# A Hymba layer on one core: one product taken apart, fillers in other PSUM tiles, a shared tile, a split reciprocal, and one hand-over between engines

## The chip, the core and the metric

The kernel runs on one core of a Trainium2 chip. The metric is device time of one execution in microseconds (us). Of each kernel there are several timed runs, of which the median counts, and one execution that was profiled.

## What is computed

One layer of a network with attention and a state-space scan side by side, over 1024 tokens of 1024 features, in float32:

```python
x = LN0(alpha*x + 0.5*SwiGLU_1(x))
u = x @ W_in            # [q | k | v | z | x_ssd | B | C | dt_fwd | dt_bwd]
a = attention(rms+rotary(q), rms+rotary(k), v)    # 8 query heads of 64, 2 key/value heads, all tokens
xs, B, C = silu(conv5(x_ssd, B, C))               # centred depthwise convolution along tokens
s = scan_forward(xs, dt_f, B, C) + scan_backward(xs, dt_b, B, C) + d_skip*xs   # chunks of 128 tokens
s = rms(s * silu(z)) * ssd_norm                   # rms over each half of 512 features
x = LN1(alpha*x + concat(a, s) @ W_out)
x = LN2(alpha*x + 0.5*SwiGLU_2(x))
x = LN3(alpha*x + sigmoid(x @ W_g + b_g) * (p @ W_p))
```

## The kernel before

**Number form.** A float32 operand is split into a high part (a rounded copy, L108 and its like) and a low part (value minus high part, L87, helper `lo`). A product is three matmuls per 128 rows of the contraction: high x low, low x high, high x high (`mm3`, L122). A 128x512 result over 1024 features takes 24 matmuls, over 512 features 12.

**Order.** TensorE (PE) executes its instructions in the order in which the code is written. On VectorE (DVE), ScalarE (ACT), GpSimd (POOL) and the DMA queue of SyncE (SP) a scheduler sets the order from the dependencies; a block marked `behind` an engine lets its instructions stand behind what that engine already has.

**PSUM.** There are two pools: `psb()` gives one of 2 tiles of 128x1024 ("big" in the profile), `pss()` one of 4 tiles of 128x512 ("sm"). A tile is free again when its last reader has run; whoever asks for a fifth small tile makes PE wait for that reader.

**Stages, in order.** FFN1 (0 to some 660 us of the span); the products of z for token rows 0 to 5; q, k, v; the convolution input, in eight steps j, inside which `ssd_prep` computes the scan's decay sums (cumulated with the triangular matrix `tri`) in two pieces; z of row 6; attention (876 to 1062 us); the backward scan and the part inside the chunks, `ssd_right` (to 1116); the forward scan, `ssd_left` (to 1183); FFN2; the gate and the end.

**Convolution.** Step j < 7 uses a big tile; step j = 7 two small ones, `p0` and `p1`, one per half of the tokens (`xbc_half`). For j < 6 the result is also needed with tokens in partitions: each half is turned by a `turn`, four PE transposes (L1026) into a small tile and an ACT copy (L1027). Turns go on a list and `pop(n)` takes n from it later. Steps j = 0 and 2 also run a piece of `ssd_prep`. There L1135 sums and L1136 transposes, for each direction d, go into the tiles `pr` and `pl`, 64 partitions and 256 columns each.

**Attention.** 64 iterations i, each a head and 128 queries: four score matmuls into a big tile (L1176), the row maximum on DVE (L1183), the exponential on ACT (L1185). Two iterations later eight PE transposes turn the probabilities into two small tiles (L1198), ACT copies their high parts (L1200), DVE forms their low parts (L87). From i = 6 on, a quarter of the product with V (L1213, L1214) runs in each iteration; after every fourth, DVE adds halves (L1221), after every eighth `normalise` takes place: DVE inverts the row sums (L1224), POOL spreads them, PE turns them (L1235), DVE multiplies (L1236), and POOL forms the high part (L1238) and the low part (L1239) of this head pair of the attention output (`a_raw`). At i = 1 `begin()` computes z's last product (row 7) with its DVE copy (L1059) and ACT exponential (L1060). What is left of it, and later the split of the first weights of the output projection, lies on the list `aside`, of which every even iteration from i = 8 on takes one: an addition of one on POOL, four reciprocals of 128 columns (L1066), a multiplication on POOL.

**Scan.** In `ssd_right` PE forms decays in big tiles (L1365); ACT's exponential (L1367), DVE's sum of the two directions (L1379), its products with C·B (L1382) and of the skip term (L1378) follow. In both scan stages PE's own work per chunk is the state's part of the result (L1287) and the new state (L1298), with DVE's L1289, L1290 and L1304 behind them. As these depend on each other, the code puts *fillers* between them: products of the output projection (`out_proj`), each a pair of 12 matmuls over 512 features for the two halves of a row's 1024 outputs, accumulated by DVE (L1483) into an SBUF tile. In `ssd_right` these are the attention halves of rows 0 to 2 (`spilled`, accumulator `accr`, loaded by DMA at L1627 and written back); in `ssd_left` those of rows 3 to 7 (`resident`) and the scan halves of rows 0 to 4 (`mixed`). `ssd_left` also turns y (L1434).

The edited lines in context:

## Time and profile before

| | |
|---|---|
| median of 3 runs | 1945.71 us (1945.52 to 1946.04) |
| the profiled execution | 1944.84 us |
| its span in the profile | 1943.0 us |
| granted TensorE clock | 0.999 of full speed |
| busy: PE / weight loads / DVE / ACT / POOL | 99% / 83% / 78% / 45% / 22% |
| chain that ended last, share of PE | 95% |
| DMA | 310 MB, 160 GB/s over the span |

A profile row gives, for a run of equal instructions, start and duration in us, the engine, the line and operation, output<-inputs by the program's names, the shape and the count (x4); in brackets the idle time of the engine ahead of it and what ended that. "PE" is the matmuls, "PEld" the weight loads beside them. PE overlaps the end of one matmul with the next, so its durations, when added, exceed the time between starts: a 128x512 matmul is shown as 0.39 us and starts come some 0.23 us apart. A line of a window gives the stretch, and then for PE, PEld, DVE, ACT and POOL the busy time with the number of instructions, the clock and DMA. A line of a group gives the instruction, its count, then busy time in all (us), the mean of one (ns), and idle time ahead.

### The profile page before, as it was taken

The page shows a single profiled execution, that of the slowest core. Times are in us where ns is not written, and L with a number is a line of the kernel's source. Part 1 is how long each engine was busy: PE and PEld are TensorE (multiplying, and loading weights), DVE is VectorE, ACT ScalarE, POOL GpSimd, SP SyncE. Part 2 cuts the span into 40 slices and gives each one's busy share as a digit, 9 for nine tenths or more (in the row PEclk, how much of TensorE's full clock was granted, in tenths as well). Part 3 has the DMA queues.
Part 4 walks back from the last instruction along what each step waited for, and adds up shares of the span by engine and source line. Part 5 has one row for each costly group of instructions (what it writes and reads, how often), then busy time and mean ns, then how long its engine had stood idle before and what let it go on. Part 6 is the DMA issues. An engine that isn't in the chain of part 4 may idle for free.

```text
span 1943.0 us, 25694 instructions
## 1 busy us (share of the span) xinstructions
PE 1930.9 (99%) x9146; PEld 1608.2 (83%) x9146; DVE 1521.0 (78%) x2357; ACT 880.9 (45%) x1509; POOL 419.7 (22%) x310
## 2 busy tenths in 40 slices
PE   9999999999999999999999999999999999999998
PEld 7888888888888889888888888888888888888886
DVE  8977777767678658758998888997786687877698
ACT  7433333324444224537887876633333333443311
POOL 0144544430001032000221001014444540001011
PEclk9999999999999999999999999999999999999999
DMA  8334554549866101241002663253544439976022
GB/s 313 127 130 152 194 180 147 195 168 380 287 221 207 64 39 53 83 123 64 6 1 77 217 224 120 93 172 143 190 170 172 179 119 352 341 261 224 30 77 97
DMA packets 147714, 310.34 MB, mean 160 GB/s; under 512 B 18129, under 2 KB 30801, under 8 KB 147585
## 3 DMA queue, kind: packets, MB, share of 16 engines
q1 hardware_dynamic: 147584, 308.69, 45.3%
q8 instruction: 72, 1.18, 0.2%
q14 instruction: 58, 0.47, 0.1%
HBM read 217.21 MB, written 91.42 MB: 159 GB/s over the span
## 4 chain that ended last, share of the span: by engine, by line
PE 95%; DVE 3%; ACT 1%; issue 1%; DMA 0%; POOL 0%; SPq 0%; DVEq 0%; ACTq 0%
PE sm L122 58%; PE big L519 12%; PE sm L519 9%; PE big L122 3%; PE big L1176 3%; PE sm L1198 2%; PE sm L1213 1%; PE sm L1214 1%; PE sm L639 1%; PE sm L1388 1%; PE sm L1287 1%; DVE nm L1183 1%; DVE conv L994 1%; PE sm L1298 0%; PE big L224 0%
## 5 line engine op out<-in xcount | busy, mean ns | idle before, releaser
L122 PE MATMUL sm<-xh,blk 128*128 128x512 f32 x1424 | 439.7, 389 | 0.0
L122 PEld LDWEIGHTS sm<-xh,blk 128*128 128x128 f32 x1424 | 267.3, 188 | 55.5
L122 PE MATMUL sm<-xl,blk 128*128 128x512 f32 x736 | 283.8, 389 | 0.0
L122 PE MATMUL sm<-blk,xl 128*128 128x512 f32 (+2 forms) x784 | 238.3, 371 | 0.2 <-ACT xn_t L1027 0.2
L122 PE MATMUL sm<-blk,xh 128*128 128x512 f32 (+2 forms) x584 | 203.3, 379 | 0.4 <-DVE accr L1483 0.3
L108 ACT CAST blk<-raw 128x512 fp32r<-128x512 f32 (+1 forms) x168 | 101.2, 610 | 214.3 <-PE sm L122 131.1
L87 DVE TENSOR_TENSOR blk<-raw,blk 128x512 fp32r<-128x512 f32 (+1 forms) x168 | 141.1, 843 | 51.8 <-ACT blk L108 51.2
L108 ACT CAST blk<-s 128x512 fp32r<-128x512 f32 x172 | 105.6, 622 | 153.1 <-PE sm L122 126.0
L87 DVE TENSOR_TENSOR blk<-s,blk 128x512 fp32r<-128x512 f32 x176 | 141.8, 809 | 40.6 <-ACT blk L108 38.5
L122 PEld LDWEIGHTS sm<-blk,xl 128*128 128x128 f32 x784 | 142.8, 188 | 24.2 <-ACT xn_t L1027 0.5
L178 POOL TENSOR_TENSOR ln_k<-ln_k,mhalf 128x1 f32<-128x1 f32 x32 | 37.4, 1174 | 578.6 <-DVE ln_k L177 562.4
L122 PEld LDWEIGHTS sm<-xl,blk 128*128 128x128 f32 x736 | 138.1, 188 | 28.6
L267 POOL TENSOR_TENSOR s<-raw 128x512 f32<-128x512 f32 x34 | 57.7, 1697 | 381.9 <-DVE blk L87 364.4
L519 PE MATMUL big<-xh 128*128 128x512 f32 x576 | 138.8, 390 | 0.0
L87 DVE TENSOR_TENSOR xh<-blk,xh 128x1024 fp32r<-128x1024 f32 x78 | 96.0, 1231 | 49.8 <-ACT xh L465 46.8
L465 ACT CAST xl<-blk 128x1024 fp32r<-128x1024 f32 x76 | 80.1, 1054 | 113.5 <-PE sm L519 43.7
L465 ACT CAST xh<-blk 128x1024 fp32r<-128x1024 f32 x78 | 82.2, 1054 | 107.5 <-PE big L519 49.0
L122 PEld LDWEIGHTS sm<-blk,xh 128*128 128x128 f32 x584 | 109.8, 188 | 20.1 <-DVE accr L1483 0.7
L519 PEld LDWEIGHTS big<-xh 128*128 128x128 f32 x576 | 107.8, 188 | 22.2
L87 DVE TENSOR_TENSOR xl<-blk,xl 128x1024 fp32r<-128x1024 f32 x76 | 92.9, 1222 | 42.4 <-ACT xl L465 34.8
L519 PE MATMUL big<-xl 128*128 128x512 f32 x480 | 115.8, 390 | 0.0
L122 PE MATMUL sm<-xET2h,blk 128*128 128x512 f32 x352 | 108.3, 389 | 0.0
(346 smaller groups left out, 4026.7 us busy)
## 6 DMA issues: line engine op xcount, KB each, us to landing
raw<-in_wi_dram SPq DMA_DIRECT2D x81, 512.0 KB
blk<-hS SPq DMA_DIRECT2D x154, 256.0 KB
hS<-h SPq DMA_DIRECT2D x88, 256.0 KB
wr<-in_wo_dram SPq DMA_DIRECT2D x44, 512.0 KB
blk<-wT SPq DMA_DIRECT2D x88, 256.0 KB
hS<-sg SPq DMA_DIRECT2D x66, 256.0 KB
wT<-wr SPq DMA_DIRECT2D x66, 256.0 KB
blk<-in_wo_dram SPq DMA_DIRECT2D x66, 256.0 KB
```

The lines of the kernel that those rows point to most:

```text
L87: (eng or self.nc.vector).tensor_tensor(out=out, in0=full, in1=hi.bitcast(F32), op=ALU.subtract)
L108: self.nc.scalar.copy(out=b[:, 0, :n], in_=src)
L122: self.nc.tensor.matmul(ps, lhsT=a, rhs=b, start=(i == 0), stop=(i == n - 1))
L178: nc.gpsimd.tensor_tensor(out=r, in0=v, in1=self.mhalf[:, :1], op=ALU.pow)
L267: lambda: G.tensor_tensor(out=s1, in0=a21, in1=a22, op=ALU.add),
L465: A.copy(out=b[:, :, 0], in_=r)
L519: nc.tensor.matmul(ps[q], lhsT=b[:, 0, x, cut], rhs=b[:, 1, y], start=j == i == 0, stop=j == NP - 1 and i == 2)
L639: nc.tensor.matmul(o, lhsT=pT[t // 4][k][:, i, c], rhs=we[n][k][:, j], start=k + i + j == 0, stop=k + i == 2)
L994: nc.vector.scalar_tensor_tensor(out=a[:, o], in0=ps[:, o.start + d - c:o.stop + d - c], scalar=cw[:, j, tap:tap + 1], in1=a[:, o], op0=AL ...
L1176: nc.tensor.matmul(ps[:, n * 512:(n + 1) * 512], lhsT=Q[:, h, q0:q0 + P], rhs=K[:, h // 4, j, n * 512:(n + 1) * 512], start=j == 0, stop=j ...
L1183: nc.vector.tensor_reduce(out=nm, in_=ps, axis=AX.X, op=ALU.max, negate=True)
L1198: nc.tensor.transpose(out=pt[:, k], in_=pr[:, kk * P:(kk + 1) * P], identity=self.ident)
```

## The change

Five edits, none of which adds or removes a matmul:

1. *z's last product* is taken apart: five of eight contraction blocks (15 matmuls) stay at i = 1, three of 3 matmuls each run in iterations 3, 4 and 5. The DVE copy and the ACT exponential come behind the last, at i = 5. The reciprocals on `aside` are eight of 64 columns instead of four of 128, so the list is four entries longer and what stands behind them comes eight iterations later.
2. *Turns* at j = 7: one behind each half product instead of two behind the second.
3. *Shared tile* in `ssd_prep`: `pl` is the second half of `pr`'s tile.
4. *Attention's last head pair*: its high part is formed by ACT and its low part by DVE, not both by POOL.
5. *Fillers* `resident(3..7)` and `mixed(0..2)` take half a big tile instead of a small one.

```diff
@@ -1004,9 +1004,10 @@
                 self.wz = [b for k in range(4) for b in self.wload(I["wz"][k])]
                 p0, p1 = self.pss(), self.pss()
                 self.xbc_half(w, xT, 0, p0)
+                self.pop()
                 conv(j, a, p0, 0, 512, 0, 512, True)
                 self.xbc_half(w, xT, 1, p1)
-                self.pop(2)
+                self.pop()
                 conv(j, a, p1, 512, 512, 0, 512, False)
                 nc.scalar.activation(out=a[:, :512], in_=a[:, :512], func=AF.Silu)
                 conv(j, a, p1, 512, 512, 512, S, True)
@@ -1053,11 +1054,22 @@
     def z_last(self, xT, aside):
 
         nc, V = self.nc, self.nc.vector
-        ps = self.z_product(NT - 1, xT)
+        ps = self.pss()
+        pairs = [(x, (w[:, 0], w[:, 1])) for x, w in zip(self.tok(xT, NT - 1), self.wz)]
+
+        def part(ks):
+            for k in ks:
+                (xh, xl), (wh, wl) = pairs[k]
+                for i, (x, w) in enumerate(((xh, wl), (xl, wh), (xh, wh))):
+                    nc.tensor.matmul(ps, lhsT=x, rhs=w, start=k == i == 0, stop=k == KD - 1 and i == 2)
+        part(range(KD - 3))
         r = self.ring.tile([P, 1024], F32, name="blk")
         z, e = r[:, :512], r[:, 512:]
-        V.tensor_copy(z, ps)
-        nc.scalar.activation(out=e, in_=ps, func=AF.Exp, scale=-1.0)
+
+        def end():
+            part((KD - 1,))
+            V.tensor_copy(z, ps)
+            nc.scalar.activation(out=e, in_=ps, func=AF.Exp, scale=-1.0)
 
         def one_more():
             nc.gpsimd.tensor_scalar(out=e, in0=e, scalar1=1.0, scalar2=None, op0=ALU.add)
@@ -1068,7 +1080,8 @@
         def silu():
             nc.gpsimd.tensor_tensor(out=z, in0=z, in1=e, op=ALU.mult)
             nc.sync.dma_start(out=self.zd[NT - 1], in_=z)
-        aside += [one_more, *(lambda m=slice(i * P, (i + 1) * P): invert(m) for i in range(4)), silu]
+        aside += [one_more, *(lambda m=slice(i * 64, (i + 1) * 64): invert(m) for i in range(8)), silu]
+        return [lambda: part((KD - 3,)), lambda: part((KD - 2,)), end]
 
 
     def ssd_prep(self, wk):
@@ -1130,7 +1143,7 @@
 
         self.sc = [self.dram.tile([2, 3, NT, 8, P], BF16, name=f"sc{i}") for i in range(2)]
         pr = self.pss()
-        pl = self.pss()
+        pl = pr[:, 256:]
         for d in range(2):
             nc.tensor.matmul(pr[0:64, d * P:(d + 1) * P], lhsT=adt[:, d].rearrange("p c h -> p (c h)"), rhs=tri[:, d], start=True, stop=True)
             nc.tensor.transpose(out=pl[0:64, d * P:(d + 1) * P], in_=ldt[:, d].rearrange("p c h -> p (c h)"), identity=self.ident)
@@ -1235,8 +1248,12 @@
                 nc.tensor.transpose(out=R[:, qt * P:(qt + 1) * P], in_=rx[:, qt].rearrange("p h d -> p (h d)"), identity=self.ident)
             nc.vector.tensor_tensor(out=raw, in0=raw, in1=R, op=ALU.mult)
             hi, lo = (x[:, hp] for x in mixT[qh][0])
-            nc.gpsimd.tensor_copy(hi, raw)
-            nc.gpsimd.tensor_tensor(out=lo, in0=raw, in1=hi.bitcast(F32), op=ALU.subtract)
+            if (qh, hp) == (1, NQ // 2 - 1):
+                nc.scalar.copy(out=hi, in_=raw)
+                self.lo(lo, raw, hi)
+            else:
+                nc.gpsimd.tensor_copy(hi, raw)
+                self.lo(lo, raw, hi, nc.gpsimd)
 
         n = 4 * len(units)
         for i in range(n + 8):
@@ -1249,7 +1266,9 @@
             if ps is not None:
                 softmax(i, ps)
             if i == 1:
-                begin()
+                late = begin()
+            if 3 <= i < 6:
+                late.pop(0)()
             for a in los:
                 self.lo(*a)
             if i >= 8 and i % 2 == 0 and aside:
@@ -1474,11 +1493,11 @@
             filler()
             turn(*w)
 
-    def out_proj(self, t, half, wm, mixT, a, ns=(0, 1)):
+    def out_proj(self, t, half, wm, mixT, a, ns=(0, 1), wide=False):
         nc = self.nc
         for n in ns:
             m = slice(n * 512, (n + 1) * 512)
-            ps = self.pss()
+            ps = self.psb()[:, :512] if wide else self.pss()
             self.mm3(ps, [(x, (w[n][:, 0], w[n][:, 1])) for x, w in zip(self.tok(mixT, t, range(half * 4, half * 4 + 4)), wm)])
             nc.vector.scalar_tensor_tensor(out=a[:, m], in0=ps, scalar=1.0 / ALPHA, in1=a[:, m], op0=ALU.mult, op1=ALU.add)
 
@@ -1593,10 +1612,11 @@
             blocks0, aside = [], []
 
             def begin():
-                self.z_last(xT, aside)
+                late = self.z_last(xT, aside)
                 early = [self.ring_raw(I["wm"][k]) for k in range(4)]
                 aside.extend(tabs)
                 aside.extend(lambda i=i, r=r: blocks0.append(self.split(r[:, i * 512:(i + 1) * 512], eng=nc.gpsimd)) for i in range(2) for r in early)
+                return late
 
             mixT = [[self.unit(h, 0)] for h in range(2)]
             with ExitStack() as c2:
@@ -1622,10 +1642,10 @@
                 blocks = blocks0
             wm[half].extend(zip(blocks[:4], blocks[4:]))
 
-        def attention_half(t, a, ns=(0, 1)):
+        def attention_half(t, a, ns=(0, 1), wide=False):
             if 0 in ns:
                 nc.sync.dma_start(out=a, in_=y0[t])
-            self.out_proj(t, 0, wm[0], mixT, a, ns)
+            self.out_proj(t, 0, wm[0], mixT, a, ns, wide)
 
         sctx = ExitStack()
         late = sctx.enter_context(tc.tile_pool(name="slate", bufs=2))
@@ -1657,7 +1677,7 @@
         def resident(t, ns=(0, 1)):
             if 0 in ns:
                 acc[t] = ap.tile([P, D], F32, name="acc1")
-            attention_half(t, acc[t], ns)
+            attention_half(t, acc[t], ns, True)
             if t == NT - 1:
                 weights(1)
 
@@ -1671,7 +1691,7 @@
                 row.st = self.small.tile([P, 4, 6], F32, name="ln_st")[:, :2]
 
             def half(row, n):
-                self.out_proj(row.t, 1, wm[1], mixT, row.a, (n,))
+                self.out_proj(row.t, 1, wm[1], mixT, row.a, (n,), row.t < 3)
                 self.ln_part(row.st, row.a, n)
 
             def root(row):
```

How this moves instructions (names as above; lines of the kernel after stand 1 to 19 higher: L1176 is L1189, L1198 L1211, L1221 L1234, L1236 L1249, L1183 L1196, L1066 L1078, L1379 L1398, L1378 L1397, L1382 L1401, L1483 L1502; z's product has the line L1064).

PE where attention starts, before: z's product ends, then scores and transposes take turns.

```order
L122 MATMUL sm<-blk,xh_5625 128x512
L122 MATMUL sm<-blk,xl_5624 128x512 x2
L122 MATMUL sm<-blk,xh_5625 128x512
L122 MATMUL sm<-blk,xl_5624 128x512
L1176 MATMUL big<-K,Q 128x512 x4
L1198 MATMUL sm<-ident,pr 128x128 x8
L1176 MATMUL big<-K,Q 128x512 x4
L1198 MATMUL sm<-ident,pr 128x128 x8
L1176 MATMUL big<-K,Q 128x512 x4
L1198 MATMUL sm<-ident,pr 128x128 x8
```

The same place after:

```order
L1064 MATMUL sm<-blk,xl_5624 128x512
L1064 MATMUL sm<-blk,xh_5625 128x512
L1064 MATMUL sm<-blk,xl_5624 128x512
L1189 MATMUL big<-K,Q 128x512 x4
L1211 MATMUL sm<-ident,pr 128x128 x8
L1189 MATMUL big<-K,Q 128x512 x4
L1211 MATMUL sm<-ident,pr 128x128 x8
L1064 MATMUL sm<-blk,xl_5624 128x512
L1064 MATMUL sm<-blk,xh_5625 128x512
L1064 MATMUL sm<-blk,xl_5624 128x512
L1189 MATMUL big<-K,Q 128x512 x4
L1211 MATMUL sm<-ident,pr 128x128 x8
```

Three matmuls of z's product stand behind each of the transposes of i = 3, 4 and 5 (the first of these groups is shown), and the product ahead of the first scores is nine shorter.

DVE inside attention around the first reciprocals, before (L1183 is the row maximum, L87 on `ptl` or `xl` a low part, L1221 the addition of halves):

```order
L1183 TENSOR_REDUCE nm<-big 128x1
L1221 TENSOR_TENSOR a_raw<-sm,a_raw 64x512
L87 TENSOR_TENSOR ptl_7809<-sm,pth_7807 128x4x128
L87 TENSOR_TENSOR ptl_7810<-sm,pth_7808 128x4x128
L1066 RECIPROCAL blk<-blk 128x128
L1183 TENSOR_REDUCE nm<-big 128x1
L87 TENSOR_TENSOR ptl_7809<-sm,pth_7807 128x4x128
L87 TENSOR_TENSOR ptl_7810<-sm,pth_7808 128x4x128
L1183 TENSOR_REDUCE nm<-big 128x1
L87 TENSOR_TENSOR ptl_7809<-sm,pth_7807 128x4x128
L87 TENSOR_TENSOR ptl_7810<-sm,pth_7808 128x4x128
L1066 RECIPROCAL blk<-blk 128x128
```

The same place after:

```order
L1196 TENSOR_REDUCE nm<-big 128x1
L1234 TENSOR_TENSOR a_raw<-sm,a_raw 64x512
L87 TENSOR_TENSOR ptl_7808<-sm,pth_7806 128x4x128
L87 TENSOR_TENSOR ptl_7809<-sm,pth_7807 128x4x128
L1078 RECIPROCAL blk<-blk 128x64
L1196 TENSOR_REDUCE nm<-big 128x1
L87 TENSOR_TENSOR ptl_7808<-sm,pth_7806 128x4x128
L87 TENSOR_TENSOR ptl_7809<-sm,pth_7807 128x4x128
L1196 TENSOR_REDUCE nm<-big 128x1
L87 TENSOR_TENSOR ptl_7808<-sm,pth_7806 128x4x128
L87 TENSOR_TENSOR ptl_7809<-sm,pth_7807 128x4x128
L1078 RECIPROCAL blk<-blk 128x64
```

Where a reciprocal of 128 columns stood every second iteration, one of 64 columns stands; the row of them is twice as long, so it runs on beyond the rows shown.

DVE at the hand-over from attention to the scan, before (L1236 is the last normalising multiplication, the next three rows the first decays of the scan, L1483 the first filler's eviction):

```order
L1221 TENSOR_TENSOR a_raw<-sm,a_raw 64x512 x2
L1236 TENSOR_TENSOR a_raw<-a_raw,sm 128x512
L1379 TENSOR_TENSOR Eb<-Eb,Ef 128x1024
L1378 TENSOR_TENSOR y<-xb,dsk 128x512 x3
L1382 TENSOR_TENSOR Eb<-Eb,cb 128x1024
L1483 SCALAR_TENSOR_TENSOR accr<-sm,accr 128x512 x2
L1301 COPY state<-sm 128x512
```

The same place after:

```order
L1234 TENSOR_TENSOR a_raw<-sm,a_raw 64x512 x2
L1249 TENSOR_TENSOR a_raw<-a_raw,sm 128x512
L1398 TENSOR_TENSOR Eb<-Eb,Ef 128x1024
L87 TENSOR_TENSOR xl_7583<-a_raw,xh_7582 128x512
L1397 TENSOR_TENSOR y<-xb,dsk 128x512 x3
L1401 TENSOR_TENSOR Eb<-Eb,cb 128x1024
L1502 SCALAR_TENSOR_TENSOR accr<-sm,accr 128x512 x2
L1320 COPY state<-sm 128x512
```

The subtraction for the low part of attention's last head pair, which POOL did, stands on DVE between L1398 (before: L1379) and L1397 (before: L1378).

## The prediction, made before the changed kernel was run

> **What bounds the kernel now.** I read the shares of busy time and the chain of work that ended last, then the list of what the tensor engine (PE) waited for, and then PE's timeline at each place that the diff touches, since a share over 1.9 ms hides stalls of half a microsecond.
>
> ```profile
> PE 1930.9 (99%) x9146; PEld 1608.2 (83%) x9146; DVE 1521.0 (78%) x2357; ACT 880.9 (45%) x1509; POOL 419.7 (22%) x310
> ...
> PE 95%; DVE 3%; ACT 1%; issue 1%; DMA 0%; POOL 0%; SPq 0%; DVEq 0%; ACTq 0%
> ```
>
> PE is busy 99% of the span and carries 95% of the chain. The change removes no matmul and adds none, so the bulk of the time stays; only moments in which PE stands or runs slower than its own rate can be won. The waits that the profile marks on PE are few:
>
> ```profile
> PE sm L1136 <- ACT xn_t L1027: 0.4, 1, 0.4
> PE sm L122 <- DVE accr L1483: 0.3, 1, 0.3
> PE big L1176 <- ACT pr L1185: 0.2, 1, 0.2
> PE sm L122 <- ACT xn_t L1027: 0.2, 1, 0.2
> ```
>
> These four (total, times, longest) add up to 1.1 us, and each lies at an edited place. They are too small a measure: PE's modelled ends overlap the next start, so a stall shows in full only from start to start. I therefore count every part by the distance of starts against the same piece of work undisturbed.
>
> **Shared tile in the preparation.** PE's timeline there:
>
> ```profile
> 809.59 0.43 PE L1135 MATMUL sm<-tri,adt 128*64 128x128 f32 x2
> 810.41 0.30 PE L1136 MATMUL sm<-ident,ldt 128*64 128x128 f32 x1 [0.39 <-ACT xn_t L1027]
> 810.64 0.43 PE L1135 MATMUL sm<-tri,adt 128*64 128x128 f32 x2
> 811.00 0.30 PE L1136 MATMUL sm<-ident,ldt 128*64 128x128 f32 x1
> ```
>
> From L1135 to L1136 it is 0.82 us the first time and 0.36 the second: 0.46 is lost while the small pool's four slots are full and ACT empties one (L1027). With `pl` in the second half of `pr` no slot is asked for. The same instructions run, and both halves are read after all of them; nothing waits for the fifth slot now. I take 0.46, bounds 0 (next need of a slot waits instead) to 0.46.
>
> **Turns apart.** At j = 7 the two turns, eight transposes, come together, and the next product finds no slot:
>
> ```profile
> 869.19 1.03 PE L1026 MATMUL sm<-ident,conv 128*128 128x128 f32 x8
> 870.46 0.50 PE L122 MATMUL sm<-blk,xl 128*128 128x512 f32 x1 [0.24 <-ACT xn_t L1027]
> ```
>
> That is 1.27 us. Eight transposes of the same shape in attention, below, take 0.79 (884.28 to 885.07). The loss is 0.48. Apart, the first turn's tile is emptied while PE runs the second half product, and only one copy is outstanding when the next product asks. ACT does the same copies, one earlier. I take 0.48, bounds 0.2 (one copy still late by the wait shown) to 0.48.
>
> **z's last product spread.** PE at the start of attention, where L1176 opens each iteration (i = 2 at 883.36, i = 7 at 894.54), and DVE inside two of these iterations:
>
> ```profile
> 883.36 1.08 PE L1176 MATMUL big<-K,Q 128*128 128x512 f32 x4
> 884.28 1.03 PE L1198 MATMUL sm<-ident,pr 128*128 128x128 f32 x8
> 885.07 1.19 PE L1176 MATMUL big<-K,Q 128*128 128x512 f32 x4
> ...
> 887.19 1.19 PE L1176 MATMUL big<-K,Q 128*128 128x512 f32 x4
> ...
> 889.38 1.21 PE L1176 MATMUL big<-K,Q 128*128 128x512 f32 x4
> ...
> 891.71 1.19 PE L1176 MATMUL big<-K,Q 128*128 128x512 f32 x4 [0.24 <-ACT pr L1185]
> ...
> 893.53 0.48 PE L1213 MATMUL sm<-pth,V 128*128 128x512 f32 x1
> ...
> 894.54 1.07 PE L1176 MATMUL big<-K,Q 128*128 128x512 f32 x4
> ```
>
> ```profile
> 886.82 1.22 DVE L1183 TENSOR_REDUCE nm<-big 128x1 f32<-128x1024 f32 x1
> 887.95 1.28 DVE L87 TENSOR_TENSOR ptl<-sm,pth 128x512 fp32r<-128x512 f32 x2
> 889.14 1.22 DVE L1183 TENSOR_REDUCE nm<-big 128x1 f32<-128x1024 f32 x1
> ```
>
> An iteration without values is 1.71 us of PE work (883.36 to 885.07), but DVE needs 2.32 for its share (886.82 to 889.14, with no gap between). So i = 3 to 5 take 885.07 to 891.71 = 6.64 instead of 3 x 1.71 = 5.13: 1.51 lost. At i = 6 the values (893.53 to 894.54, 1.01) bring PE to 2.72; it takes 2.83, 0.11 more lost. In all 1.62. The change carries nine matmuls of 0.23 (four scores take 0.92) into i = 3, 4, 5: PE has 1.71 + 0.69 = 2.40 per iteration against DVE's 2.32, and DVE no longer sets the pace. What it adds: z's sum holds one of the four small slots for four iterations more, and its DVE copy and ACT exponential fall at i = 5 instead of i = 1, when DVE is loaded; a 128x512 operation of that kind is 0.68 on DVE (the L1483 row below). DVE recovers 2.72 - 2.32 = 0.40 per iteration from i = 6, so that copy is a lag of two iterations, of which the two score tiles absorb part. I deduct 0.30, nearer to nothing than to the whole 0.68. Gain 1.3; bounds 0.9 (the copy in full) to 1.6.
>
> **Eight reciprocals of 64 columns for four of 128.** Groups of DVE in attention, and two stretches of eight iterations (busy and instructions of PE, PEld, DVE, ACT, POOL): i = 15 to 22, where the reciprocals end, and i = 23 to 30, with the same work and none of them:
>
> ```profile
> L1066 DVE RECIPROCAL blk<-blk 128x128 f32<-128x128 f32 x4 | 3.8, 938 | 0.0
> ...
> L1224 DVE RECIPROCAL rinv<-rsum 128x8 f32<-128x8 f32 x8 | 1.6, 195 | 0.0
> ```
>
> ```profile
> 916.45:939.92 23.47, 23.14 (x133) 18.92 (x132) 22.99 (x31) 19.18 (x36) 3.78 (x4) 1.00 0.03 12
> 939.92:962.17 22.25, 22.25 (x133) 19.02 (x132) 21.12 (x29) 19.40 (x36) 3.72 (x4) 1.00 0.00 1
> ```
>
> The stretch with the last reciprocals is 23.47 - 22.25 = 1.22 us longer. (938 - 195) / 120 columns = 6.2 ns a column, so a 64-column one is 195 + 56 x 6.2 = 542 ns, and eight are 4.3 us against 3.8: the work on DVE grows by 0.6, or by 0.3 if the ends overlap the next start as they do elsewhere (1.28 shown for two L87 in a distance of 1.19). But DVE's block between two reductions falls from 0.94 to 0.54, and the eight are spread over 16 iterations instead of 8. A stretch with four of them needs 21.12 + 4 x 0.54 = 23.28 by busy time, more than 22.25. By back-to-back work it is 8 x 2.32 = 18.6, plus some 1.9 for normalising, plus 4 x 0.47 = 1.9, or 22.4: hardly over. I take the second count, for DVE worked without gaps at 2.32 where it was the bound, and leave a residue of 0.3: gain 0.9, bounds 0.2 (the first count, 1.03 over) to 1.2.
>
> The Trainium skill (Perfetto Trace Analysis, Optimizing Scalar/DVE Operations) gives about 60 ns of overhead per DVE instruction on SBUF and says to group operations where the engine is saturated, and to break them up where it isn't saturated but makes others wait. By that figure four more instructions are an estimated 0.24 us of DVE, near the 0.3 to 0.6 above. As DVE is busy 21.12 of 22.25 before any reciprocal, its first half speaks against the edit: by it this term would be about nothing and the sum 0.9 smaller. The result under that rule is the second rival.
>
> **Attention's last parts off GpSimd.** POOL, DVE and PE at the hand-over:
>
> ```profile
> 1056.97 1.29 POOL L1239 TENSOR_TENSOR xl<-a_raw,xh 128x512 fp32r<-128x512 f32 x1
> ...
> 1065.31 2.38 POOL L1239 TENSOR_TENSOR xl<-a_raw,xh 128x512 fp32r<-128x512 f32 x1
> ```
>
> ```profile
> 1065.30 1.23 DVE L1379 TENSOR_TENSOR Eb<-Eb,Ef 128x1024 f32<-128x1024 f32 x1 [0.75 <-ACT Eb L1367]
> 1067.73 1.90 DVE L1378 TENSOR_TENSOR y<-xb,dsk 128x512 f32<-128x512 f32 x3 [1.20 <-POOL xl L1239]
> ...
> 1071.35 1.29 DVE L1483 SCALAR_TENSOR_TENSOR accr<-sm,accr 128x512 f32<-128x512 f32 x2 [0.59 <-DMA accr<-y]
> ```
>
> ```profile
> 1070.81 1.03 PE L1298 MATMUL sm<-xs,xb 128*128 128x256 f32 x4
> 1072.10 0.50 PE L122 MATMUL sm<-blk,xh 128*128 128x512 f32 x1 [0.27 <-DVE accr L1483]
> ```
>
> POOL's subtraction ends at 1067.69 (elsewhere it takes 1.29; here L1379 runs beside it). On it hang DVE's L1378 and the load of `accr`, hence the eviction at 1071.35 and PE at 1072.10. After the change ACT casts the high part when its L1367 ends (about 1065.3; ended by 1065.9), and DVE subtracts behind L1379, at 1066.5 to 1067.1: the load and the eviction come 0.6 earlier. PE could have started when the four L1298 were through: eight of that shape take 1.72 between 1137.52 and 1139.24 in the rows below, so four end 0.86 behind 1070.81, at 1071.67. It gains 0.43 of the 0.6; bounds 0.27 (the marked wait) to 0.43.
>
> **Fillers in big tiles.** Second phase of the scan, PE and DVE (L1287 and, left out behind it, L1298 are the scan's own, four each; L1434 transposes y; L122 is the filler):
>
> ```profile
> 1137.52 1.02 PE L1287 MATMUL sm<-state,bc 128*128 128x256 f32 x4
> ...
> 1139.24 0.60 PE L1434 MATMUL sm<-ident,y 128*128 128x128 f32 x4
> 1139.94 0.50 PE L122 MATMUL sm<-blk,xh 128*128 128x512 f32 x1
> ...
> 1147.28 0.60 PE L1434 MATMUL sm<-ident,y 128*128 128x128 f32 x4
> 1147.63 0.48 PE L122 MATMUL sm<-blk,xh 128*128 128x512 f32 x1
> ```
>
> ```profile
> 1139.20 0.68 DVE L1483 SCALAR_TENSOR_TENSOR acc<-sm,acc 128x512 f32<-128x512 f32 x1
> ```
>
> At 1139.94 the filler waited until DVE's eviction of 1139.20 gave a small slot: 0.70 from L1434 against 0.35 at 1147.28, so 0.35 lost, and none such in the next turn. In a big tile the filler doesn't compete for it. Gain 0.35, bounds 0 to 0.35. What the two big slots cost instead is the third rival.
>
> **The sum.** 0.46 + 0.48 + 1.3 + 0.9 + 0.43 + 0.35 = 3.92. DVE's order also changes in the scan, where evictions of fillers and an addition of the state trade places; the waits of PE on an eviction that exist before are 0.2 to 0.4 each, and I set 0.4 against one or two new ones (bounds 0 to 0.8). Gain 3.5 us. The profiled execution took 1944.84 (span 1943.0, 1.8 around it), so it would be 1941.3; the median of the runs, 1945.71, stands 0.87 above it, and I give 1942.2 for the median.
>
> **Rivals.**
> First, everything goes: no residue and no new wait. 0.46 + 0.48 + 1.62 + 1.22 + 0.43 + 0.35 = 4.56, time 1941.1. For it: every stall has one named releaser. Against: z's copy has to go somewhere on a loaded DVE.
> Second, DVE stays the bound of attention: the eight reciprocals take 0.6 more of it, the copy of z lands at i = 5, so that term gives 0.2 and the spread 0.9, and the waits cost 0.4: 0.46 + 0.48 + 0.9 + 0.2 + 0.43 + 0.35 - 0.4 = 2.4, time 1943.3. For it: 21.12 of 22.25. Against: DVE worked at 2.32 an iteration without a gap.
> Third, slower: the big pool has two tiles, so a filler must be evicted before the next but one begins. Turns are 7.69 apart (1139.94 to 1147.63), a product is 12 x 0.23 = 2.7, so the eviction has 5.0 us. The product that ended at 1137.52 was out at 1139.88, 2.4 behind. It decides from a lag of 5.0: DVE would have to be 2.6 later. There are 16 such products; to be slower by 3.9 us over the 3.5 gained each would have to wait 0.46, time 1949.6 and above. Only a DVE order that puts evictions last in each turn does that.
> Fourth, the freed time is given back, because attention and the scan are paced by DVE or a load further on: gain 0 to 1.4, time 1944.3 to 1945.7. For it: DVE is the releaser in most of the rows above. Against: the turn after 1147.28 and the stretch after 939.92 run without a loss as soon as the cause is gone.
>
> **Chances.** Forecast 0.55; everything goes 0.2; DVE stays the bound 0.16; given back 0.06; slower 0.03. The range 1940.9 to 1944.4 takes in the first rival with 0.2 to spare and the second with half of its gain lost again (1.2), and leaves out most of the fourth and the third. A change of 0.2%, 3.89 us, is about what a measurement of this kernel can tell from none; it lies at 1941.82, a little beyond the forecast. Faster by more: the first rival and a quarter of the forecast, 0.35; within 0.62; slower 0.03.
>
> **What would show it.** Right: no wait on ACT L1027 in PE's list; iterations 3 to 5 about 2.40 apart; stretches of eight iterations within 0.3 of 22.25 while reciprocals run; the second phase's filler 0.35 behind its transposes every time; the load of `accr` starting near 1067.1 less what came before. Wrong: iterations 6 to 9 above 2.8 (z's copy), stretches of 23 (reciprocals), or PE waiting for an eviction of a big tile.

## The result, and the profile after

| | before | after |
|---|---|---|
| median | 1945.99 us (8 runs, 1944.51 to 1946.46) | 1940.18 us (8 runs, 1940.07 to 1940.51) |
| the profiled execution | 1944.84 us, span 1943.0 | 1940.12 us, span 1938.3 |

The ratio is 0.9971, 95% interval 0.9960 to 0.9982: 5.8 us or 0.3% faster, clear of no change, below the predicted range (1940.9 to 1944.4) and 2.0 under the predicted 1942.2. Between the two traces it is 4.7 us. Two later executions of the kernel before, of 2144.75 and 9667.75 us, fell far out of the rest and enter no ratio and no spread below.

The page of the kernel after: span, shares and the chain.

```profile
span 1938.3 us, 25689 instructions
...
PE 1927.8 (99%) x9146; PEld 1607.8 (83%) x9146; DVE 1523.9 (79%) x2362; ACT 881.6 (45%) x1510; POOL 417.2 (22%) x308
...
PE 99%; DVE 0%; DMA 0%; ACT 0%; DVEq 0%; issue 0%; SPq 0%
```

The list of what PE waited for is now one line, at the start of the kernel:

```profile
PE big L634 <- DVE s L631: 1.2, 1, 1.2
```

PE carries 99% of the chain instead of 95%; DVE's 3% are gone. Where the time came from is read by setting equal matmuls of the two traces side by side: PE of the kernel after is ahead by 0.48 us at its 20th matmul (before any edit), 0.95 at 812 us, 1.43 at 872, 2.56 at 916 (in attention, behind z's product), 3.71 at 947 (behind the reciprocals), 4.16 at 1076, 4.33 at 1117 and 4.73 at 1144, and no more from there. So the edited places give 4.25 and the start 0.48.

PE at the shared tile, then at the turns:

```profile
809.09 0.43 PE L1148 MATMUL sm<-tri,adt 128*64 128x128 f32 x2
809.45 0.30 PE L1149 MATMUL sm<-ident,ldt 128*64 128x128 f32 x1
809.68 0.43 PE L1148 MATMUL sm<-tri,adt 128*64 128x128 f32 x2
810.05 0.30 PE L1149 MATMUL sm<-ident,ldt 128*64 128x128 f32 x1
...
868.71 0.60 PE L1027 MATMUL sm<-ident,conv 128*128 128x128 f32 x4
869.06 0.47 PE L122 MATMUL sm<-blk,xl 128*128 128x512 f32 x1
```

0.36 both times instead of 0.82 and 0.36; the four transposes left take 0.35 and the product follows.

PE at iterations 5 to 7 of attention (they open at 886.67, 889.15 and 892.12), and DVE there:

```profile
886.67 1.08 PE L1189 MATMUL big<-K,Q 128*128 128x512 f32 x4
...
889.15 1.08 PE L1189 MATMUL big<-K,Q 128*128 128x512 f32 x4
890.07 1.03 PE L1211 MATMUL sm<-ident,pr 128*128 128x128 f32 x8
891.12 0.47 PE L1226 MATMUL sm<-pth,V 128*128 128x512 f32 x1
...
892.12 1.08 PE L1189 MATMUL big<-K,Q 128*128 128x512 f32 x4
```

```profile
889.14 0.68 DVE L87 TENSOR_TENSOR ptl<-sm,pth 128x512 fp32r<-128x512 f32 x1
889.74 0.68 DVE L1071 COPY blk<-sm 128x512 f32<-128x512 f32 x1
890.34 0.68 DVE L87 TENSOR_TENSOR ptl<-sm,pth 128x512 fp32r<-128x512 f32 x1
```

Iteration 5 takes 2.48 (iterations 3 and 4: 2.57 and 2.49; 2.40 was forecast), and PE works through it. Iteration 6, 889.15 to 892.12, takes 2.97 instead of 2.72: the values (L1226) begin 1.05 behind the transposes where 0.79 would do, because z's copy (L1071) stands on DVE between the two low parts that they need.

The stretches of eight iterations i = 15 to 22 and i = 23 to 30, four reciprocals in the first and two in the second; and the group of the reciprocals:

```profile
913.89:936.14 22.25, 22.25 (x133) 19.02 (x132) 22.16 (x33) 18.97 (x35) 2.49 (x3) 1.00 0.00 1
936.14:958.46 22.32, 22.32 (x134) 19.00 (x133) 21.72 (x31) 19.17 (x36) 3.74 (x4) 1.00 0.04 13
```

```profile
L1078 DVE RECIPROCAL blk<-blk 128x64 f32<-128x64 f32 x8 | 4.3, 537 | 0.0
```

DVE does 0.5 us more for the reciprocals (4.3 against 3.8), is busy for 22.16 of 22.25, and PE loses nothing.

PE at the first filler of the scan, and at the filler behind the first transposes of y:

```profile
1067.09 1.03 PE L1317 MATMUL sm<-xs,xb 128*128 128x256 f32 x4
1067.95 0.50 PE L122 MATMUL sm<-blk,xh 128*128 128x512 f32 x1
```

```profile
1134.92 0.60 PE L1453 MATMUL sm<-ident,y 128*128 128x128 f32 x4
1135.27 0.48 PE L122 MATMUL big<-blk,xh 128*128 128x512 f32 x1
```

0.86 instead of 1.29, and 0.35 instead of 0.70.

### The profile page after: what moved, and what is told of

The parts are those of the page before. It is cut to its first block, busy times and chain, and to the rows that moved or that the text cites. A ratio compares the mean times of both kernels' runs of the same rounds, so it can differ in the third digit from the quotient of the medians.

```text
span 1938.3 us, 25689 instructions
## 1 busy us (share of the span) xinstructions
PE 1927.8 (99%) x9146; PEld 1607.8 (83%) x9146; DVE 1523.9 (79%) x2362; ACT 881.6 (45%) x1510; POOL 417.2 (22%) x308
## 4 chain that ended last, share of the span: by engine, by line
PE 99%; DVE 0%; DMA 0%; ACT 0%; DVEq 0%; issue 0%; SPq 0%
PE sm L122 56%; PE big L519 12%; PE sm L519 9%; PE big L122 6%; PE big L1189 3%; PE sm L1211 3%; PE sm L1226 2%; PE sm L1227 1%; PE sm L639 1%; PE sm L1407 1%; PE sm L1306 1%; PE sm L1317 1%; PE big L1722 0%; PE big L926 0%; PE big L224 0%; PE sm L224 0%
## 5 line engine op out<-in xcount | busy, mean ns | idle before, releaser
L122 PE MATMUL sm<-blk,xl 128*128 128x512 f32 (+2 forms) x704 | 208.1, 369 | 0.0
L87 DVE TENSOR_TENSOR blk<-raw,blk 128x512 fp32r<-128x512 f32 (+1 forms) x168 | 142.5, 852 | 53.8 <-ACT blk L108 53.2
L87 DVE TENSOR_TENSOR blk<-s,blk 128x512 fp32r<-128x512 f32 x176 | 142.3, 812 | 39.6 <-ACT blk L108 36.8
L122 PE MATMUL sm<-blk,xh 128*128 128x512 f32 (+2 forms) x448 | 158.0, 373 | 0.0
L122 PEld LDWEIGHTS sm<-blk,xl 128*128 128x128 f32 x704 | 127.8, 188 | 20.6
L87 DVE TENSOR_TENSOR xh<-blk,xh 128x1024 fp32r<-128x1024 f32 x78 | 95.3, 1222 | 52.1 <-ACT xh L465 46.1
L87 DVE TENSOR_TENSOR xl<-blk,xl 128x1024 fp32r<-128x1024 f32 x76 | 92.9, 1222 | 43.1 <-ACT xl L465 40.8
L122 PE MATMUL sm<-xET3h,blk 128*128 128x512 f32 x352 | 108.3, 389 | 0.0
```

The costliest lines, as they stand in the source:

```text
L87: (eng or self.nc.vector).tensor_tensor(out=out, in0=full, in1=hi.bitcast(F32), op=ALU.subtract)
L122: self.nc.tensor.matmul(ps, lhsT=a, rhs=b, start=(i == 0), stop=(i == n - 1))
```

## The experiments

Each kernel ran five rounds beside the kernel before, whose medians there were 1945.31 to 1945.54 (24 to 33 runs). The interval of each ratio to before is 0.08% to 0.12% to either side (1.6 to 2.3 us), since the runs of before spread by 2.4 to 2.9 us; kernels that are closer than that are compared by their medians, with the trace beside them. The sessions ran on four chips, and the medians of before differ by 0.2 between them.

**The two kernels again.** No edit.

> The kernel before, run again for its trace. The eight timed runs of it lie 1.1 us above its profiled execution (1945.99 against 1944.84), those of the changed kernel 0.1 (1940.18 against 1940.12). Theory A (the surplus is outside the change, at the start of the kernel, where PE begins its first product 0.48 us later in the trace of before than in the one of after): 1945 to 1946, and the trace shows the surplus ahead of 20 us and nowhere else. Theory B (the surplus lies at a place that the change edits, and comes and goes there): the trace, if it is one of the slower executions, is over 1 us behind the first trace of before inside 800 to 1190 us.

> The changed kernel again, to stand beside the others on one chip and to give a second trace. Theory B2 (the kernel before loses 0.35 to 1.1 us at the filler behind y's first transposes, more or less from execution to execution, since DVE's queue there holds work that waits for loads; the big tiles take PE out of that queue): 1940.2 again, 5.1 below before, the runs within some 0.6 of one another where those of before spread over 2.5, and no stall at a filler in the trace. Theory A2 (the parts are worth what the first two traces show, 4.2 beside the start): 4.2 below before.

The kernel before: 1945.33 (ratio 1.0, 0.9992 to 1.0009). The kernel after: 1940.13 (0.9972, 0.9961 to 0.9983), 5.4 below before on that chip; its runs spread by 1.3, not 0.6. The second trace of before is the key to the surplus. Its start is 0.69 earlier than in the first trace, its span still 0.4 longer: it loses 1.03 more at two of the edited places, as theory B had it. PE at the first filler and behind the transposes of y, and DVE (first the row of the first trace of before, then the row of the second):

```profile
1071.66 0.50 PE L122 MATMUL sm<-blk,xh 128*128 128x512 f32 x1 [0.47 <-DVE accr L1483]
...
1138.80 0.60 PE L1434 MATMUL sm<-ident,y 128*128 128x128 f32 x4
1140.32 0.50 PE L122 MATMUL sm<-blk,xh 128*128 128x512 f32 x1 [0.92 <-DVE acc L1483]
```

```profile
1128.21 0.69 DVE L1458 TENSOR_TENSOR y<-y,zs 128x512 f32<-128x512 f32 x1 [2.40 <-DMA y<-yd]
```

```profile
1128.52 0.69 DVE L1458 TENSOR_TENSOR y<-y,zs 128x512 f32<-128x512 f32 x1 [3.16 <-DMA y<-yd]
```

From the transposes to the filler it is 1.52 instead of 0.70, and at the first filler the wait is 0.47 instead of 0.27. PE came to the transposes 0.44 earlier than in the first trace, but DVE's eviction, for which the filler waits, came 0.38 later (1139.58 against the 1139.20 shown in the prediction). The load of y, for which DVE stood at 1128, landed 0.31 later, but one row further DVE is only 0.16 behind (1129.08 and 1129.24). The last wait that the profile marks on DVE ahead of the eviction is for ACT's cast of weights, and from there DVE is 0.39 behind (first trace, then second):

```profile
1133.45 0.69 DVE L87 TENSOR_TENSOR blk<-raw,blk 128x512 fp32r<-128x512 f32 x1 [0.54 <-ACT blk L108]
```

```profile
1133.84 0.69 DVE L87 TENSOR_TENSOR blk<-raw,blk 128x512 fp32r<-128x512 f32 x1 [0.77 <-ACT blk L108]
```

ACT in turn stood for loads (0.82 and 1.04; the cast waits for several at once, and which one decides is not shown). SP issues them behind the loads of y, in the second trace 0.45 to 0.48 later; the row is the first of the weights (first trace, then second):

```profile
1127.42 0.43 SPq L1619 DMA_DIRECT2D raw<-in_wm_dram  x1
```

```profile
1127.90 0.43 SPq L1619 DMA_DIRECT2D raw<-in_wm_dram  x1
```

So two of the stalls that the change takes away end with loads, and were at their shortest in the trace from which they were priced.

**One part undone at a time.**

```diff
# u_z: product whole at i = 1, four reciprocals of 128     # u_spread: only the first, u_recip: only the second
-        part(range(KD - 3))
+        part(range(KD))
-        aside += [one_more, *(lambda m=slice(i * 64, (i + 1) * 64): invert(m) for i in range(8)), silu]
+        aside += [one_more, *(lambda m=slice(i * P, (i + 1) * P): invert(m) for i in range(4)), silu]
# u_turns
-                self.pop()           # behind the first half product
...
+                self.pop(2)          # behind the second
# u_shared
-        pl = pr[:, 256:]
+        pl = self.pss()
# u_hand
-            if (qh, hp) == (1, NQ // 2 - 1):
+            if False:
# u_wide: wide=False for every filler
```

> The changed kernel with z's last product in one piece at i = 1 and four reciprocals of 128 columns, as before; the other edits stay. Theory A (separate stalls, each worth what the two traces show at its place): 1.1 + 1.15 us slower than the changed kernel, about 1942.4, PE's iterations i = 3 to 5 again 2.1 to 2.3 apart, the stretch of eight with the last reciprocal 1.2 longer. Theory B (one part carries the surplus of 1.1 to 1.6 us that the timed runs show over the traces, and attention is the likeliest): about 1943.7.

> The changed kernel with z's last product in one piece at i = 1, but eight reciprocals of 64 columns. Theory A: 1.1 to 1.4 slower (iterations 3 to 5 paced by DVE), 1941.4, and no loss while the reciprocals run. Rival (DVE's lag from iterations 3 to 6 is what the reciprocals trip over later, so the spread alone is worth both): 1942.4.

> The changed kernel with four reciprocals of 128 columns, the product spread. Theory A: PE stands at i = 14 to 18 as before, 1.15 slower: 1941.3. Rival (the loss there came from the lag that DVE carried out of iterations 3 to 6, and the shorter reciprocals give nothing): 1940.2.

> The changed kernel with both turns behind the second half product at j = 7. Theory A (separate stalls): PE waits for ACT's copy again, 0.43 to 0.48 slower: about 1940.65. Rival (the later stage takes it up): 1940.2. Theory B (the surplus hangs on this part): 1941.7.

> The changed kernel with a tile of its own for pl. Theory A: 0.46 slower, about 1940.65, and the 0.82 between L1148 and L1149 back. Rival (the wait of the next stage absorbs it): 1940.2. Theory B: 1941.7.

> The changed kernel with attention's last high and low part on POOL again. Theory A: POOL's subtraction runs beside DVE's sum of two SBUF tiles, takes some 2.4 us, and PE stands 0.43 at the eviction of the first filler: about 1940.6. Rival (what waits is the accumulator's load whatever frees it): 1940.2.

> The changed kernel with all fillers in small tiles again. Theory A: the stalls at the filler behind y's first transposes (0.35) and ahead of the scan's second half (0.2) come back: about 1940.7. Theory B: if the surplus hangs on the fillers, about 1942. Rival (the big tiles give nothing, DVE's other order did it): 1940.2.

| undone | median | slower than 1940.15 by | behind the trace of after at that place |
|---|---|---|---|
| shared tile | 1940.47 | 0.3 | 0.45 |
| turns | 1940.95 | 0.8 | 0.49 |
| hand-over | 1941.05 | 0.9 | 0.40, with its follower 0.57 |
| spread | 1941.21 | 1.1 | 1.0 |
| reciprocals | 1941.43 | 1.3 | 1.3 |
| spread and reciprocals | 1942.58 | 2.4 | 2.4 |
| fillers | 1941.45 | 1.3 | 1.0 |

The five parts make 0.3 + 0.8 + 0.9 + 2.4 + 1.3 = 5.7 against 5.3 for all of them. The kernel after did not run on the chips of this table; reckoned from the kernel before beside each, every part is some 0.2 larger and the sum 6.9 against 5.4. So the parts add up to within 1.5 us, and spread and reciprocals simply add. That a part is worth the same without the others was tried for two alone (below). The rivals by which DVE's lag from the start of attention would carry the loss at the reciprocals (u_spread at 1942.4, u_recip at 1940.2) fell. What PE waited for in these kernels, the row at the undone place (u_spread, u_recip, u_turns, u_hand, u_wide):

```profile
PE big L1189 <- ACT pr L1198: 0.3, 1, 0.3
```

```profile
PE sm L1211 <- DVE xh L87: 0.3, 2, 0.2
```

```profile
PE sm L122 <- ACT xn_t L1027: 0.2, 1, 0.2
```

```profile
PE sm L122 <- DVE accr L1502: 0.2, 1, 0.2
```

```profile
PE sm L122 <- DVE acc L1502: 0.7, 1, 0.7
```

The stall of the first filler also has a follower. In the trace of u_hand PE falls another 0.17 behind by 1113 us, which is the difference that the first two traces show between 1076 and 1117; no fillers' tile is concerned there, since with small tiles it does not come back, and the hand-over alone, on the kernel before, brings it (0.17 in the trace of x_hand). With the hand-over the first filler starts 0.68 to 0.99 behind the matmuls ahead of it (L1317 above) in the traces, and 1.32 in v1, where PE comes there earlier; without it 1.24 to 1.50.

**One part done alone, on the kernel before.** The same lines, the other way.

> The kernel before with the fillers in big tiles and nothing else. Theory B2: 0.7 to 1.2 faster than before (1944.2 to 1944.6 where before is 1945.3), and no stall at the filler behind y's first transposes. Theory A2: 0.35 faster. Rival (evictions of big tiles come late and PE waits at the next but one filler): not faster, and a wait of L122 on L1483's big tile in the trace.

> The kernel before with the hand-over alone changed (last high part on ACT, low part on DVE). Theory C: PE gets the 0.43 to 0.64 that it stood at the first eviction in the two traces of before, and gives part of it back at the filler behind y's transposes, which waits for a load: 0.1 to 0.5 faster, 1944.9 to 1945.3. Rival (separate stalls): 0.5 faster and the stall there as before.

Fillers in big tiles alone: 1944.35 (0.9994, 0.9985 to 1.0003), 1.2 below before; in the trace the filler behind y's transposes comes 0.36 behind them, while the first filler, still in a small tile, stands 0.4 as before. The hand-over alone: 1944.43 (0.9995, 0.9986 to 1.0004), 1.1 below: more than either expectation. Both intervals take in no change, so it is the medians and the traces that speak. In the trace of the hand-over PE stands at neither the first filler nor ahead of the scan's second half (0.39 and 0.17 won on the first trace of before), but behind y's transposes the filler comes after 1.12, where the two traces of before have 0.70 and 1.52:

```profile
PE sm L122 <- DVE acc L1487: 0.5, 1, 0.5
```

So beside the first trace 0.43 of the 0.56 is given back there, as theory C had it, and beside the second trace nothing is. The way from y's transposes to the filler is 0.36 in every trace with big tiles; with small ones it is 0.70 and 1.52 (before), 1.12 here, 1.31 (u_wide) and, below, 1.07 (x_early), 1.65 (u_wide_pool) and 0.36 (u_wide_early). The 0.70 from which the prediction priced it is the mildest of those with a stall.

**What makes the eviction late.** Three kernels: with small tiles, the low parts of the second weights on POOL; with small tiles, y of chunks 0 and 1 loaded from an array that is ready early; and the latter on the kernel before. The two kernels with the early load leave out the layer's own y of these chunks.

```diff
# u_wide_pool (on u_wide)
-                        blocks += [self.split(h) for h in halves]
+                        blocks += [self.split(h, eng=nc.gpsimd) for h in halves]
# u_wide_early (on u_wide), x_early (on before)
-            nc.sync.dma_start(out=y, in_=self.yd[ch])
+            nc.sync.dma_start(out=y, in_=(self.zd if ch < 2 else self.yd)[ch])
```

> The changed kernel with all fillers in small tiles, and the low parts of the second half's weights on POOL instead of DVE. With small tiles alone it was 1941.4, 1.2 slower than the changed kernel, with PE 0.97 late at the filler behind y's first transposes. If DVE is late there because its queue holds low parts of weights, for which ACT's casts wait behind a load: the stall falls below 0.3 and the time to about 1940.5. Rival (DVE has too much to do there whatever it waits for; two low parts are 1.2 of it, so it may also be the work itself): the queue shows no idle time ahead of these rows but still ends as late, 1941.4.

> The changed kernel with all fillers in small tiles and the y of chunks 0 and 1 loaded from z's array (those two chunks' y is not the layer's). Theory C: the 1.2 us that small tiles cost against the changed kernel (1941.4 against 1940.15) go for the most part: 1940.3 to 1940.7. Rival (five small tiles a turn are too few for four slots whatever the load does): 1941.4, with PE late at the same filler.

> The kernel before, with the y of chunks 0 and 1 in the forward scan loaded from z's array (written long before) instead of what the backward scan has just written; those two chunks' y is therefore not the layer's. Theory C (the eviction that PE waits for at the filler behind y's first transposes is late because DVE waits for that load, 2.40 and 3.16 us idle ahead of the multiplication with z's gate in the two traces of before): the idle time goes, the stall there falls from 0.35 to 1.1 to below 0.2, and the time by 0.4 to 1.0 from 1945.4. Rival (DVE's own work and order set it): no change, 1945.4.

With the low parts on POOL it was 1944.32, 2.9 slower than small tiles alone. POOL takes 1.3 to 1.75 for one of them, the power that DVE needs for the next chunk's normalisation (L136) stands behind it, and DVE waits for that:

```profile
1132.39 1.25 DVE L129 TENSOR_TENSOR rs_t<-yr 128x2 f32<-128x2 f32 x1 [1.86 <-POOL yr L136]
```

That run says nothing for or against DVE's own low parts as the cause; it made another wait. Of the 3.0 by which its trace is behind that of u_wide, 0.8 arise up to this filler and 2.2 only between 1155 and 1160, where PE waits 0.3 for one of these low parts and then 1.4 for weights of FFN2. With the early load and small tiles it was 1940.41 instead of 1941.45, near the kernel after, and no wait of PE behind y's transposes is left in its trace: there the late load of y is the cause, itself or through the loads that SP issues behind it. On the kernel before, the early load gave 1944.31, 1.2 below before (0.9984 to 1.0001), but its trace, of its slowest run (1944.99), still has the stall, a wait of 0.5, though DVE starts y's multiplication 4 us sooner. There DVE stands later, for a cast of weights:

```profile
1124.01 0.69 DVE L1458 TENSOR_TENSOR y<-y,zs 128x512 f32<-128x512 f32 x1 [1.24 <-DMA y<-zd]
...
1133.48 0.69 DVE L87 TENSOR_TENSOR blk<-raw,blk 128x512 fp32r<-128x512 f32 x1 [2.14 <-ACT blk L108]
```

A last wait of 0.3, for ACT, follows just ahead of the eviction. A wait for that cast, a shorter one, was the last in the two traces of before, too. So several loads reach PE through the order of DVE's queue; y's is only one of them. How much of the surplus in the untraced executions each of them has stays open.

**Two more edits, and what they gave back.** v1 puts z's copy behind both low parts and the sums turned at i = 63 into a big tile; v3 also opens the pool of the first fillers' accumulator ahead of its neighbours.

```diff
# v1
-            if 3 <= i < 6:
-                late.pop(0)()
             for a in los:
                 self.lo(*a)
+            if 3 <= i < 6:
+                with self.behind(mybir.EngineType.Activation), self.behind(mybir.EngineType.DVE):
+                    late.pop(0)()
...
-            R = self.pss()
+            R = self.psb()[:, :512] if wide else self.pss()      # normalise(i == n - 1)
# v3: self.accr = c.enter_context(...) moved ahead of ep and two
```

> The changed kernel with two more edits: z's copy at i = 5 stands on DVE behind both low parts of that iteration instead of between them, and the row sums that are turned at i = 63 go into a big tile. In the trace after, values at i = 6 start 0.26 late because the second low part comes behind z's copy, and the transposes after the turned sums 0.31 late because they find no small tile. If both readings hold: 0.5 faster than the changed kernel, 1939.7. Rival for the first: the copy then delays the next row maximum and PE stands one iteration later, nothing gained. Rival for the second: DVE's low part comes late whatever the tile, nothing gained.

> The kernel with z's copy behind both low parts and the turned sums of i = 63 in a big tile, and the pool of the first fillers' accumulator opened ahead of the two others of the backward scan, so that it takes other memory than attention's last a_raw. There PE was 0.56 earlier in attention and lost 0.46 of it again at the eviction into that accumulator, whose load waits until a_raw is free. If that dependency is what gives it back: no wait of PE on accr, 0.4 less, 1939.5. Rival (another tile now lies on a_raw and waits): the same or slower, 1939.9 to 1941.

v1: 1939.91 (6 runs) beside 1940.13 of the kernel after (7 runs) in the same session: a version that may beat both, by less than these runs can tell. In its trace both readings hold, 0.25 at i = 6 and 0.52 at i = 63; its start is 0.21 later, so PE leaves attention 0.56 earlier. Then it stands again:

```profile
PE sm L122 <- DVE accr L1503: 0.3, 1, 0.3
PE sm L1307 <- DVE state L1324: 0.2, 1, 0.2
```

From start to start that is 0.46 and 0.39: the first waits for the accumulator's load, the second for DVE behind casts of weights, for whose load ACT stood 0.9. Here, then, won time is given back at waits that end with a load.

v3 removed the first of these and was 4.3 slower than v1, 1944.23 (0.9993, 0.9984 to 1.0002), outside both of its expectations. Its trace is of its slowest run (1946.52). The loads of the next accumulator are now issued at 1118 us instead of 1102, DVE waits for them, and PE for the eviction of a big tile:

```profile
1123.50 1.29 DVE L1503 SCALAR_TENSOR_TENSOR acc<-big,acc 128x512 f32<-128x512 f32 x2 [3.06 <-DMA acc<-y]
```

```profile
PE big L122 <- DVE acc L1503: 3.2, 1, 3.2
```

```profile
1115.00:1120.00 5.00, 5.00 (x24) 4.18 (x23) 0.94 (x2) 5.00 (x22) 0.00 (x0) 1.00 0.42 130
1120.00:1124.20 4.20, 1.04 (x5) 0.57 (x3) 1.14 (x3) 3.41 (x15) 0.00 (x0) 0.87 0.92 318
1124.20:1129.70 5.50, 5.45 (x13) 4.30 (x14) 3.22 (x7) 2.83 (x12) 1.10 (x1) 0.50 1.04 395
1129.70:1135.00 5.30, 5.30 (x25) 4.43 (x24) 4.18 (x12) 0.61 (x3) 0.70 (x1) 0.98 1.05 387
```

The windows of v3 (busy time of PE, PEld, DVE, ACT, POOL; then the granted clock and DMA) show the wait in the second and, in the third, a clock of 0.50: 13 matmuls where the fourth has 25. The third rival's mechanism exists, with two tiles and a late eviction; in this trace one such wait cost 3.6 us, and the half clock behind it 2.5 more, from start to start beside v1. The median of v3 is 2.3 below this run; what the wait costs there is not shown.

## Why the prediction was wrong, point by point

- **The bound** was right: PE throughout, only its stalls to win; each of the six came out faster and none slower. No rival came true: the first (everything goes, 1941.1) was nearest, and still 0.9 too slow.
- **Shared tile, 0.46; turns, 0.48:** 0.48 and 0.48 between the traces (0.3 and 0.8 by medians). Right.
- **Spread, 1.3:** 1.1. The residue is where it was put, z's copy, with 0.25 against 0.30; beyond that iterations 3 to 5 took 2.48 to 2.57, not 2.40.
- **Reciprocals, 0.9:** 1.15 between the traces, 1.3 by undoing. The 0.3 set aside was not needed. The list of waits had a fifth row at an edited place that the prediction did not show, L1198 on DVE's low part (0.2); it is this term's, as u_recip shows. The first count there (21.12 + 4 x 0.54 = 23.28 of busy time against 22.25) is refuted by the stretch with four reciprocals, which takes 22.25 with DVE "busy" for 22.16: busy times overlap at the ends, and the count by distances, 22.4, was the better one. The Trainium skill (Perfetto Trace Analysis, Optimizing Scalar/DVE Operations) would have engines that are saturated do fewer, larger operations; the 0.5 us of added work is twice the 0.24 estimated from its overhead, the loss that this rule foretold did not come, and its other half, breaking up what makes others wait, is what the trace shows.
- **Hand-over, 0.43:** 0.45 at the first filler, and 0.17 at a follower that had no term. By medians 0.9 to 1.1.
- **Fillers, 0.35:** this is the term that was mis-sized. 0.35 was one execution; 0.95 with small tiles again, 1.17 in the second trace of before, 1.2 to 1.3 by medians. The prediction read the eviction as the releaser and did not follow it back to the loads for which DVE and ACT had stood, which would have warned of a stall that changes from execution to execution.
- **New waits, 0.4:** none came. The moved rows of DVE held nobody up.
- **From the profiled execution to the median, 0.87 added:** the largest error. It took the distance as a constant. After the change it is 0.06 (1940.18 against 1940.12): the load-bound stalls of before, longer in the second trace than in the first, are among those that the change removes. So this and the fillers' term are one failed step: the stall was priced at its length in one execution, and what the other executions had beyond that was carried over as if it would stay.

The sum of it: 0.87 less the 0.06, 0.4, 0.25 (reciprocals), 0.17 (follower), 0.48 at the start, which belongs to no edit and is the chance of these two traces, and 0.2 the other way (spread) account for 1.9 of the 2.0 us. That the 0.87 sits in the load-bound stalls is shown for two traces (0.21 and 0.82 between them, at the two places) and supported by the parts' medians and by the other traces with small tiles; the other executions left no trace.

## What to carry to other kernels

Before pricing a stall from one trace, follow its releaser back: if that engine itself stood for a load, the stall is a sample, and the median can hold two to four times as much (here 0.9 to 1.1 for 0.43, and 1.2 to 1.3 for 0.35). A distance between the profiled run and the median may be such stalls too, and then it goes with them. Whether a nearly busy engine can take more, count by the distances of its back-to-back instructions and not by its busy time.

## What the runs showed of the hardware

- A wait of 3.2 us cost PE its clock: in v3 the granted clock was 0.50 for the next 5.5 us, and 128x512 matmuls started 0.43 apart instead of 0.23. The wait of 0.92 in the second trace of before left it at 1.00 (the window behind it, last below), and so did one of 1.4 in u_wide_pool. The Trainium skill (TensorE: Matmul & The Clock Gate, What's actually happening) gives half rate after an idle window of some 3.4 us and full rate after a busy one of that length; the trace agrees on the half and on the order of the time, with 5.7 us of matmuls until full rate. The half came before a whole idle time of that length: the window of 0.87 above puts it 1.1 us before 1124.20 (0.13 x 2 x 4.20), which is some 2.0 behind the modelled end of PE's last matmul, 1121.05:

```profile
1120.02 1.03 PE L1318 MATMUL sm<-xs,xb 128*128 128x256 f32 x4
1124.25 0.80 PE L122 MATMUL big<-blk,xh 128*128 128x512 f32 x1 [3.20 <-DVE acc L1503]
```

And behind the wait of 0.92:

```profile
1140.40:1145.40 5.00, 5.00 (x22) 4.13 (x23) 4.92 (x13) 3.92 (x16) 0.69 (x1) 1.00 0.82 276
```

- The start of the kernel differs between executions of the same instructions by more than several of these edits are worth: PE's 20th matmul started between 7.2 and 8.3 us in the traces of this study. What differs is how long the first matmuls of 128x512 start 0.43 apart: up to 6.3 us in the first trace of before, up to 5.0 in that of after, and 0.22 apart from there.
- A low part of 128x512 took POOL 1.3 to 2.4 us against 0.68 on DVE, the longest when DVE worked on two operands from SBUF beside it.
